# Two-layer mixer network on one core: full-row score corrections, scaling on VectorE alone, a copy moved to ScalarE, and a shorter program end

## The chip, the cores and the metric

The kernel runs on one core of one Trainium2 chip. The metric is the device time of the whole program in microseconds (us). TensorE is called PE here, VectorE DVE, ScalarE ACT, GpSimd POOL, and SyncE, which issues the loads, SP.

## What is computed

256 tokens of width 1024 pass through two layers. Layer 0 mixes the tokens with stick-breaking attention and an S5 state-space model, layer 1 with a sparse attention of 16 heads (4 groups of keys and values, head width 64). After each mixer there is a layer norm, a mixture of 16 experts of which each token uses 2, and another layer norm. The change touches the attention of layer 1:

```
s = q @ ks.T * scale, masked           # "selected" branch, causal here
p = softmax(s);  o_s = p @ vs
s = q @ kw.T * scale, masked           # "window" branch, causal here
p = softmax(s);  o_w = p @ vw
o = g[0] * o_c + g[1] * o_s + g[2] * o_w    # g = sigmoid(gate), one per token, head and branch
out = o @ w_out
```

With 256 tokens every block of 64 keys is selected and the window covers all keys, so both branches are plain causal softmax attention.

## The kernel before

Weights stream from DRAM as tiles of 128x2048 (1 MB) into a pool of `u` buffers, in one fixed order, through SP's DMA queue. A load starts when a `u` buffer is free; the same pool also holds intermediate tiles. The order of instructions on each engine is fixed when the program is built, from the order in which the code issues them and from priorities; at run time each engine executes its own list strictly in order and waits on semaphores for the others.

In `mixer1`, matrices are multiplied in a split form: a value x is written as a rounded part and a remainder, and products of the parts are added. A head has 64 rows (half c of the 128 partitions holds its rounded q, the other half the remainder of q). `kk` holds the rounded keys in both halves, so one matmul over 128 rows adds two of the products, and `kl` the remainders of the keys, in the 64 rows of half c alone. `head(i, c)` does one of 16 heads; i counts eight pairs. For each half t of the queries (128 rows) it takes one PSUM tile `acc` (four of them exist in rotation), and issues three matmuls: q by `kk` (L1504), 64 rows of q by `kl` (L1505), and the causal mask by an identity (L1506). For t = 0 the scores of the two branches are 2 x 128 columns, for t = 1 they are 2 x 256. DVE takes the row maxima (L1507), ACT exponentiates each branch and adds up its rows (L1510), DVE inverts the sums (L1513), multiplies them by the gates (L1515), and the probabilities are scaled: those of t = 0 on DVE (L1522), those of t = 1 on POOL (L1519), by `PSC`.

`turn_p(h)`, two heads later, transposes the scaled probabilities on PE (L1529, L1535) into PSUM tiles `mm`. DVE copies the first (L1530), ACT the second (L1536), into the tile `PT` of the pair, a `u` buffer. `values(i)`, two heads after the second turning, multiplies `PT` by the values (L1550, 16 matmuls), adds the compressed branch (L1553), and ACT and DVE write the two parts of the result to `oT` (L1555, L1556). `attend` interleaves these steps, with other jobs of the layer during the first heads.

At the end of the program (`body`) all engines load a count of tokens (L1726) and pass an `If` (L1728): when an expert has more tokens than fit, the whole network is computed again in a full form. With these inputs the count is below the limit, so each engine jumps over the second network. L1741 in the trace stands for the program's own end.

Of the kernel before, what the change touches and what calls it, by code (L numbers as in the profile page):

```python
# [38 lines left out]
WARM0 = 5  # L39
WARM2 = 2  # L40
LAG = 2
PSC = (lambda h: False, lambda h: True)
OV = 3
LATE = (8, 10)
LATE_S = 11
# [6 lines left out]
class K:  # L52
# [17 lines left out]
    def restart(self, full):  # L70

        self.full = full
        self.plan, self.tiles, self.late, self.late_s, self.in_s, self.last = [], [], [], [], [], []
        self.left = []
        self.issued = self.used = 0
        self.cap = 0
        self.rest = self.n0 = None
        self.mark = None
        self.loads = None
        self.behind = self.cut = self.tail = None  # L80
        self.staged, self.to_split, self.ahead = [], 0, 2
# [49 lines left out]
    def issue(self, cap=None):  # L131

        self.cap = self.cap if cap is None else cap
        while self.issued < len(self.plan):
            if self.issued - self.used - sum(self.used <= i < self.issued for i in self.left) >= self.cap:
                break
            if self.issued in self.left:
                self.tiles.append(None)
                self.issued += 1
                continue  # L140
            t = (self.s if self.issued in self.in_s else self.u)()
            n = 1024 if self.issued in self.last else 2048
            for c in range(0, 2048, n):
                d = self.loads = self.nc.sync.dma_start(t[:, c:c + n], self.plan[self.issued][:, c:c + n])
                if self.mark is not None:
                    self.follow(d, self.mark)
            self.tiles.append(t)
            self.issued += 1

    def issue_late(self):  # L150

        i = self.late.pop(0)
        self.tiles[i] = [self.b2() for _ in range(4)]
        for j, t in enumerate(self.tiles[i]):
            self.nc.sync.dma_start(t, self.plan[i][:, j * 512:j * 512 + 512])

    def issue_s(self):

        i = self.late_s.pop(0)
        self.tiles[i] = t = self.s()  # L160
        self.nc.sync.dma_start(t, self.plan[i])

    def unit(self):
        t = self.tiles[self.used]
# [60 lines left out]
    def pack(self, name, dt, parts, t=None):  # L225

        if t is None:
            t = self.const.tile([P, sum(math.prod(sh) for sh in parts)], dt, name="c_" + name)
            setattr(self, name, t)
        d = self.nc.sync.dma_start(t, self.a[name])  # L230
        if self.loads is not None:
            self.follow(d, self.loads)
        o, r = 0, []
        for sh in parts:
            m = math.prod(sh)
            v = t[:, o:o + m]
            if len(sh) > 1:
                ax = "abcd"[:len(sh)]
                v = v.rearrange(f"p ({' '.join(ax)}) -> p {' '.join(ax)}", **dict(zip(ax, sh)))
            r.append(v)  # L240
            o += m
        return r
# [95 lines left out]
    def ln_transpose(self, li, n, store=None):  # L338

        nc = self.nc  # L340
        hT = self.u([P, KC, T])
        for k in range(KC):
            pt = self.acc() if k in (4, 5) else self.mm()
            for t in range(2):
                nc.tensor.transpose(pt[:, t * P:(t + 1) * P], n[:, t, k * P:(k + 1) * P], self.ident)
            self.scaled(hT[:, k], pt[:, 0:T], li, k, k % 2)
            if store is not None and k % 2:
                nc.sync.dma_start(store[:, k - 1:k + 1], hT[:, k - 1:k + 1])
        return hT

    def scaled(self, o, x, li, k, on_act):
# [305 lines left out]
    def s5_tables(self, load_x, room):  # L657
# [4 lines left out]
        small = lambda t, j: t[:, j * 512:j * 512 + 512].rearrange("p (a r h) -> p a r h", a=NP, r=2)  # L662
        par = us[:, 1344:1392].rearrange("p (x a) -> p x a", x=3)
        c8 = us[:, 1392:1424]
        nc.sync.dma_start(us[:, 1344:1424], self.a["s5_par"])
        load_x()
        bc = ua[:, 0:1024].rearrange("p (x a r h) -> p x a r h", x=2, a=NP, r=2)
        nc.sync.dma_start(bc, self.a["s5_bc"])
        lr, li, ldt = par[:, 0], par[:, 1], par[:, 2]
        cols = us[:, 0:960].rearrange("p (n a) -> p n a", a=NP)  # L670
        ints = us.bitcast(I32)[:, 1424:1456].rearrange("p (n a) -> p n a", a=NP)
# [185 lines left out]
    def s5_kernel(self, ca, bd):  # L857

        nc, s5 = self.nc, self.s5
        nc.gpsimd.memset(bd, 0.0)  # L860
        for g in range(2):
            s = slice(g * 64, g * 64 + 64)
            nc.scalar.activation(bd[s, :, :, g * 16:g * 16 + 16], s5["bb"][s], AF.Copy)
        pk = self.mm()
        for k4 in range(4):
            for ri in range(2):
                for q in range(4):
                    pr = k4 * 4 + q
                    nc.tensor.matmul(pk[q * 32:q * 32 + 32, k4 * P:k4 * P + P], bd[:, pr, ri],
                                     ca[ri][:, pr].rearrange("p d h -> p (d h)"), start=(ri == 0), stop=(ri == 1),  # L870
                                     skip_group_check=True, tile_position=(0, q * 32))
        ks = self.b2([P, 4, P])
        nc.scalar.activation(ks.rearrange("p k n -> p (k n)"), pk, AF.Copy)
        nc.gpsimd.tensor_tensor(ks[:, :, 0:16], ks[:, :, 0:16], self.s5dd, ALU.add)
        kds = []
        for kh in range(2):
            kd = self.drp.tile([16, 16, P], F32, name=f"kd{kh}")
            nc.sync.dma_start(kd.rearrange("h (g k) n -> g h (k n)", g=8),
                                ks[:, kh * 2:kh * 2 + 2].rearrange("p k n -> p (k n)"))
            kds.append(kd)  # L880
        return kds

    def s5_toeplitz(self, kds, kts):

        for kt, kd in zip(kts, kds):
            for j in range(8):
                n = 16 * (8 - j)
                self.nc.sync.dma_start(kt[j * 16:j * 16 + 16, :, P - n:P], kd[:, :, 0:n])

    def s5_transpose(self, x, o):  # L890

# [176 lines left out]
    def mixer0(self):  # L1068
# [5 lines left out]

        def load_x():
            t = self.u()
            half = lambda c: nc.sync.dma_start(t[:, c * 1024:c * 1024 + 1024], self.plan[0][:, c * 1024:c * 1024 + 1024])
            for k in range(0, KC, 2):
                nc.sync.dma_start(xT[:, k:k + 2], self.a["xT"][:, k:k + 2])
                if k == 0:  # L1080
                    half(0)
            half(1)
# [18 lines left out]
        def u_out(j):  # L1101
            def f(ps):
                nc.scalar.activation(uS[:, :, j], ps[:, 0:T].rearrange("p (c i) -> p i c", i=8), AF.Copy)
                if j == 3:
                    ud = self.drp.tile([8, P, P], F32, name="ud")
                    nc.sync.dma_start(ud.rearrange("j a n -> a j n"), uS.rearrange("p j k c -> p j (k c)"))
                    nc.sync.dma_start(U.rearrange("p g k c -> p (g k c)"), ud.rearrange("j (h g) n -> (j h) (g n)", h=16))
            return f

        bbp = [self.u([P, 16, 8, 16]) for _ in range(2)]  # L1110
# [190 lines left out]
    def mixer1(self, hT):  # L1301
# [43 lines left out]
        kk = self.u([P, 2, 2, 2, T], F32R)  # L1345
        vh = self.u([P, 2, 1024])
        V = vh[:, 0].rearrange("p (t n) -> p t n", t=2)
        kl = [self.b2((P, 2, T), F32R) for _ in range(2)]
        rows = (slice(0, 64), slice(64, P))

        turned = {}
# [4 lines left out]
        def k_turn(t):  # L1356
            pt = self.turn(turned["k", t]).rearrange("p (b j) n -> p j b n", b=2)
            n = slice(t * P, t * P + P)
            for c, s in enumerate(rows):
                nc.scalar.activation(kk[s, c, :, :, n], pt[s], AF.Copy)  # L1360
                for j in range(2):
                    v.tensor_tensor(kl[j][s, :, n], pt[s, j], kk[s, c, j, :, n].bitcast(F32), ALU.subtract)
                nc.scalar.activation(kk[rows[1 - c], c, :, :, n], pt[s], AF.Copy)

        js = [self.job_T(xs, window(i)) for i in (1, 2, 3)] + self.jobs_tok(xs, k_out, self.acc)
# [121 lines left out]
        hd = {}  # L1487

        def head(i, c):
            j, s = i // 4, slice(c * 64, c * 64 + 64)  # L1490
            h = i * 2 + c
            if c == 0:
                hd["PT"] = self.u()
            PT = hd["PT"][:, 0:1536].rearrange("p (c b n) -> p c b n", c=2, b=2)[:, c]
# [4 lines left out]
            for t in range(2):  # L1499
# [2 lines left out]
                z3 = z[:, 0:2 * n].rearrange("p (b n) -> p b n", b=2)  # L1502
                q = qq[j][:, c, i % 4, t * P:t * P + P]
                nc.tensor.matmul(z3, q, kk[:, c, j, :, 0:n], start=True, stop=False, skip_group_check=True)  # L1504
                nc.tensor.matmul(z3, q[s], kl[j][s, :, 0:n], start=False, stop=False, skip_group_check=True)  # L1505
                nc.tensor.matmul(z3[:, :, t * P:t * P + P], self.identb, self.caus, start=False, stop=True, skip_group_check=True)  # L1506
                v.tensor_reduce(mx[:, 2 * t:2 * t + 2], z3, AX.X, ALU.max, negate=True)  # L1507
                p_ = self.b2((P, 2, T)) if t else p0
# [2 lines left out]
                                         accum_out=sm[:, 2 * t + b:2 * t + b + 1])  # L1511
                pr.append(p_)
            v.reciprocal(sm, sm)  # L1513
            s2 = sm.rearrange("p (t b) -> p t b", t=2)
            v.tensor_tensor(s2, s2, gt[:, :, h, 1:3], ALU.mult)  # L1515
            for t in range(2):
                x, n, pool = pr[t], P * (t + 1), PSC[t](h)
                if pool:
                    nc.gpsimd.tensor_tensor(x, x, sm[:, 2 * t:2 * t + 2, None].broadcast_to([P, 2, n]), ALU.mult)  # L1519
                    continue  # L1520
                for b in range(2):
                    v.tensor_scalar(x[:, b], x[:, b], sm[:, 2 * t + b:2 * t + b + 1], None, ALU.mult)  # L1522
            hd[h] = (pr, PT)

        def turn_p(h):
            pr, PT = hd[h]
            pt = self.mm()
            for b in range(2):
                nc.tensor.transpose(pt[:, b * P:b * P + P], pr[0][:, b, 0:P], self.ident)  # L1529
            v.tensor_copy(PT[:, :, 0:P], pt[:, 0:T].rearrange("p (b n) -> p b n", b=2))  # L1530
            pt = self.mm()
            for b in range(2):
                for kb in range(2):
# [188 lines left out]
def body(ctx, tc, a, out):  # L1722
# [2 lines left out]
    network(k, a, out)  # L1725
    v = nc.values_load(k.mxi[0:1, 0:1], min_val=0, max_val=T,  # L1726
                       skip_runtime_bounds_check_because="a count of tokens, only compared")
    with tc.If(v > LIMIT):  # L1728

        k.restart(True)  # L1730
        network(k, a, out)
# [20 lines left out]
```

## Time and profile before

| | |
|---|---|
| time, three runs | 756.63, 756.65, 759.73 us (median 756.65) |
| profiled execution | 759.68 us, of which 757.8 us is the span of the trace |
| busy: PE, DVE, ACT, POOL | 733.8 us (97%), 333.1 (44%), 207.5 (27%), 46.8 (6%) |
| granted clock of PE over the span | 0.991 |
| heads of mixer1 in the trace | first score 426 us, last values 495 us |
| matrices moved | 238 MB read, mean 317 GB/s |

The profile gives the busy time of each engine and the share of the span. A busy PE is not a PE at its peak: a matmul counts as busy from its start to its modelled end, and neighbours overlap, so the cost of one is read as the step from the end of the one before it to its own end.

### The profile page before, as it was taken

What the parts mean: (1) busy time and instruction counts of PE and PEld (TensorE: products, weight loads), DVE (VectorE), ACT (ScalarE), POOL (GpSimd) and SP (SyncE); (2) the same over time, 40 slices, a digit from 0 to 9 for tenths busy, and PEclk for the clock granted to TensorE, in tenths of its full rate; (3) what the DMA queues carried; (4) which work ended last, traced back from release to release, by engine and by line L of the source; (5) the groups of instructions that cost most, each with busy time, mean ns of one, the idle gap of its engine ahead of it and who ended that gap; (6) DMA issues with size and microseconds to landing.
All of it is one profiled execution on the core that took longest, in us unless ns stands there. A gap on an engine that the chain in (4) does not pass through costs nothing. (4 is left out here: it accounts for less than half of the span.)

```text
span 757.8 us, 10531 instructions
## 1 busy us (share of the span) xinstructions
PE 733.8 (97%) x4115; PEld 413.9 (55%) x4115; DVE 333.1 (44%) x849; ACT 207.5 (27%) x422; POOL 46.8 (6%) x45
## 2 busy tenths in 40 slices
PE   7999999999999999999999999999999999999993
PEld 6588777634334335334878665687535335343332
DVE  9995667512112112115855897835212112221123
ACT  1345443212101001003534675732211001011002
POOL 2010000002000000000020241300002000000000
PEclk9999999999999999999999998999999999999998
DMA  8838999799999999999982100398799999999941
GB/s 321 299 119 147 398 372 402 256 347 387 381 425 421 421 422 421 420 416 422 420 338 106 57 1 1 135 387 308 233 376 395 393 421 421 422 420 421 421 185 60
DMA packets 42539, 241.00 MB, mean 318 GB/s; under 512 B 8144, under 2 KB 9680, under 8 KB 15568
## 3 DMA queue, kind: packets, MB, share of 16 engines
q1 hardware_dynamic: 42480, 240.23, 80.7%
q8 instruction: 34, 0.56, 0.3%
q14 instruction: 25, 0.20, 0.1%
HBM read 238.38 MB, written 1.84 MB: 317 GB/s over the span
## 5 line engine op out<-in xcount | busy, mean ns | idle before, releaser
L493 PE MATMUL mm<-u,s 128*64 128x512 f32 x960 | 214.3, 595 | 0.0
L493 PEld LDWEIGHTS mm<-u,s 128*64 128x64 f32 x960 | 66.7, 137 | 129.6 <-issue 122.3
L523 PE MATMUL mm<-u,b 128*64 128x512 f32 x512 | 113.1, 593 | 0.0
L528 ACT ACTIVATE b<-mm,gslot 128x512 fp32r<-128x512 f32 x32 | 22.0, 687 | 259.0 <-PE mm L523 259.0
L529 DVE SCALAR_TENSOR_TENSOR b<-mm,gslot,b 128x512 fp32r<-128x512 f32 x32 | 24.0, 751 | 146.2 <-ACT b L528 146.2
L523 PEld LDWEIGHTS mm<-u,b 128*64 128x64 f32 x512 | 36.3, 137 | 72.0 <-issue 70.8
L195 DVE TENSOR_TENSOR s<-u,s 128x1024 fp32r<-128x1024 f32 x37 | 45.8, 1248 | 27.9 <-ACT s L192 26.3
L572 DVE TENSOR_TENSOR b<-b,mm 128x256 f32<-128x256 f32 x32 | 12.0, 417 | 92.0 <-PE mm L493 92.0
L192 ACT ACTIVATE s<-u 128x1024 fp32r<-128x1024 f32 x37 | 38.7, 1056 | 42.0 <-PE acc L205 28.9
L986 PE MATMUL mm<-u,u 128*128 128x256 f32 x208 | 46.7, 382 | 2.5 <-DMA u<-w_in 2.4
L986 PEld LDWEIGHTS mm<-u,u 128*128 128x128 f32 x208 | 38.9, 190 | 9.6 <-issue 2.4
L354 ACT ACTIVATE s<-mm,c_k_all 128x256 f32<-128x256 f32 x32 | 18.1, 564 | 81.8 <-PE mm L469 81.8
L469 PE MATMUL mm<-b,u 128*128 128x256 f32 x160 | 39.0, 325 | 0.0
L203 PE MATMUL acc<-s,u 128*128 128x512 f32 x96 | 38.0, 396 | 0.5 <-ACT u L1206 0.5
L205 PE MATMUL acc<-s,u 128*128 128x512 f32 x96 | 37.8, 394 | 0.0
L204 PE MATMUL acc<-s,u 128*128 128x512 f32 x96 | 37.5, 391 | 0.0
L534 PE MATMUL acc<-b,b 128*128 128x512 f32 x128 | 33.6, 399 | 0.1
L469 PEld LDWEIGHTS mm<-b,u 128*128 128x128 f32 x160 | 29.9, 190 | 6.4 <-issue 4.9
L592 DVE COPY b<-mm 128x512 f32<-128x512 f32 x16 | 11.1, 692 | 46.4 <-PE mm L591 46.2
L356 DVE TENSOR_SCALAR s<-mm,c_k_all 128x256 f32<-128x256 f32 x32 | 16.8, 542 | 22.9 <-PE mm L469 22.7
L534 PEld LDWEIGHTS acc<-b,b 128*128 128x128 f32 x128 | 22.5, 189 | 8.0 <-issue 3.2
L469 PE MATMUL mm<-b,s 128*128 128x256 f32 x96 | 23.5, 286 | 0.0
(312 smaller groups left out, 998.8 us busy)
## 6 DMA issues: line engine op xcount, KB each, us to landing
u<-moe SPq DMA_DIRECT2D x180, 1024.0 KB, 12.5
u<-w_in SPq DMA_DIRECT2D x26, 1024.0 KB, 16.2
u<-w_in SPq DMA_DIRECT2D x10, 512.0 KB, 6.9
s<-moe SPq DMA_DIRECT2D x4, 1024.0 KB, 5.7
b<-moe SPq DMA_DIRECT2D x16, 256.0 KB, 8.1
u<-moe SPq DMA_DIRECT2D x8, 512.0 KB, 16.9
u<-xT SPq DMA_DIRECT2D x4, 256.0 KB, 5.6
out<-u SPq DMA_DIRECT2D x4, 256.0 KB, 4.4
```

What stands on the lines that cost most here:

```text
L192: a = self.nc.scalar.activation(s[:, 0], x, AF.Copy)
L195: self.mark = self.nc.vector.tensor_tensor(s[:, 1], x, s[:, 0].bitcast(F32), ALU.subtract)
L203: mm(o, l[0], r[0], start=first, stop=False, skip_group_check=True)
L204: mm(o, l[0], r[1], start=False, stop=False, skip_group_check=True)
L205: self.tail = mm(o, l[1], r[0], start=False, stop=last, skip_group_check=True)
L469: nc.tensor.matmul(pg[:, 0:T], x[:, t, k * P:(k + 1) * P], g.bitcast(F32) if m == 1 else g, start=(i == 0), stop=(i == 2 * m - 1))
L493: self.mark = nc.tensor.matmul(h[c * 64:(c + 1) * 64], xe[:, k, e + c], w[c], start=(k == 0), stop=(k == KC - 1))
L523: self.mark = nc.tensor.matmul(y[c * 64:(c + 1) * 64], hx[:, f, c * 64:(c + 1) * 64], w[:, c * 512:c * 512 + 512], start=(f == 0), stop=(f ...
L528: nc.scalar.activation(yh, y, AF.Copy, scale=gs)
L529: nc.vector.scalar_tensor_tensor(yl, y, gs, yh.bitcast(F32), ALU.mult, ALU.subtract)
L534: self.tail = nc.tensor.matmul(out[half][t], sT[:, t * P:(t + 1) * P], yy, start=False, stop=(p == 7 and j == 1), skip_group_check=True)
L986: self.mark = self.nc.tensor.matmul(ps, w[:, k * P:k * P + P], xT[:, k], start=(k == 0), stop=(k == KC - 1))
```

## The change

Five edits. (1) `kl` becomes one full `u` tile: like `kk` it has 128 rows for each c, of which POOL sets the 64 rows of the other half to zero, and L1505 multiplies all 128 rows of q. The remainders are formed by four DVE instructions instead of eight. (2) `PSC`, the scaling on POOL and the product of the inverted sums and gates are gone: DVE scales all four blocks of a head, each with two scalars, the inverted sum and the gate. (3) The first turned probabilities are copied to `PT` by ACT instead of DVE. (4) Loads and stores of the full form of the network go through POOL's queue, so that SP has next to nothing in that branch. (5) The `If` no longer prefers to fall through into its body, which puts the block for the other case next after the main program.

```diff
-PSC = (lambda h: False, lambda h: True)
...
         self.full = full
+        self.q = self.nc.gpsimd if full else self.nc.sync
...
-                d = self.loads = self.nc.sync.dma_start(t[:, c:c + n], self.plan[self.issued][:, c:c + n])
+                d = self.loads = self.q.dma_start(t[:, c:c + n], self.plan[self.issued][:, c:c + n])
...
-        kl = [self.b2((P, 2, T), F32R) for _ in range(2)]
+        kl = self.u([P, 2, 2, 2, T], F32R)
+        for c in range(2):
+            nc.gpsimd.memset(kl[(1 - c) * 64:(1 - c) * 64 + 64, c].bitcast(F32), 0.0)
...
-                for j in range(2):
-                    v.tensor_tensor(kl[j][s, :, n], pt[s, j], kk[s, c, j, :, n].bitcast(F32), ALU.subtract)
+                v.tensor_tensor(kl[s, c, :, :, n], pt[s], kk[s, c, :, :, n].bitcast(F32), ALU.subtract)
...
-                nc.tensor.matmul(z3, q[s], kl[j][s, :, 0:n], start=False, stop=False, skip_group_check=True)
+                nc.tensor.matmul(z3, q, kl[:, c, j, :, 0:n], start=False, stop=False, skip_group_check=True)
...
-            s2 = sm.rearrange("p (t b) -> p t b", t=2)
-            v.tensor_tensor(s2, s2, gt[:, :, h, 1:3], ALU.mult)
             for t in range(2):
-                x, n, pool = pr[t], P * (t + 1), PSC[t](h)
-                if pool:
-                    nc.gpsimd.tensor_tensor(x, x, sm[:, 2 * t:2 * t + 2, None].broadcast_to([P, 2, n]), ALU.mult)
-                    continue
                 for b in range(2):
-                    v.tensor_scalar(x[:, b], x[:, b], sm[:, 2 * t + b:2 * t + b + 1], None, ALU.mult)
+                    v.tensor_scalar(pr[t][:, b], pr[t][:, b], sm[:, 2 * t + b:2 * t + b + 1], gt[:, t, h, 1 + b:2 + b],
+                                    ALU.mult, ALU.mult)
...
-            v.tensor_copy(PT[:, :, 0:P], pt[:, 0:T].rearrange("p (b n) -> p b n", b=2))
+            nc.scalar.activation(PT[:, :, 0:P], pt[:, 0:T].rearrange("p (b n) -> p b n", b=2), AF.Copy)
...
-    with tc.If(v > LIMIT):
+    with tc.If(v > LIMIT, preferred_fallthrough_block=False):
```

The order of instructions shifts too. On ACT, between the turning of head 3 and the exponentials of heads 4 and 5, the list reads before (L1510 exponentials, L1536 the copy of the second turned tile, of head 2 at the top and of head 3 at the bottom, L1555 the copy of the first values):

```order
L1536 ACTIVATE u_3196<-mm_3323 128x2x256
L1510 ACTIVATE u_3296,sm_560_3298<-acc_3299,mx_559_3297 128x128 x2
L1510 ACTIVATE b_563_3311,sm_560_3298<-acc_3306,mx_559_3297 128x256 x2
L1555 ACTIVATE u_2877<-mm_3329 128x256
L1510 ACTIVATE u_3296,sm_568_3342<-acc_3343,mx_567_3341 128x128 x2
L1510 ACTIVATE b_571_3355,sm_568_3342<-acc_3350,mx_567_3341 128x256 x2
L1536 ACTIVATE u_3196<-mm_3367 128x2x256
```

and now (L1525 is the new copy, L1531 the old L1536, L1550 the old L1555):

```order
L1525 ACTIVATE u_3193<-mm_3316 128x2x128
L1531 ACTIVATE u_3193<-mm_3320 128x2x256
L1525 ACTIVATE u_3193<-mm_3360 128x2x128
L1531 ACTIVATE u_3193<-mm_3364 128x2x256
L1510 ACTIVATE u_3293,sm_559_3295<-acc_3296,mx_558_3294 128x128 x2
L1510 ACTIVATE b_562_3308,sm_559_3295<-acc_3303,mx_558_3294 128x256 x2
L1550 ACTIVATE u_2874<-mm_3326 128x256
L1510 ACTIVATE u_3293,sm_567_3339<-acc_3340,mx_566_3338 128x128 x2
```

Both copies of head 3 now stand ahead of the exponentials of head 4; before, its one copy stood behind those of heads 4 and 5.

PE, at the same place, turns head 3 and goes on to the scores of head 6. Before (L1529 and L1535 are the turning, `acc_3376` the first scores of head 6):

```order
L1506 LDWEIGHTS c_k_bits
L1506 MATMUL acc_3350<-c_k_bits 128x2x128
L1529 MATMUL mm_3363<-c_k_all,u_3196 128x128 x2
L1535 MATMUL mm_3367<-c_k_all,b_548_3243 128x128 x4
L1504 MATMUL acc_3376<-u_2582,u_2875 128x256
L1505 MATMUL acc_3376<-b_454_2584,u_2875 128x256
```

and now (L1524 and L1530 are the turning):

```order
L1506 LDWEIGHTS c_k_bits
L1506 MATMUL acc_3347<-c_k_bits 128x2x128
L1524 MATMUL mm_3360<-c_k_all,u_3193 128x128 x2
L1530 MATMUL mm_3364<-c_k_all,b_547_3240 128x128 x4
L1504 MATMUL acc_3373<-u_2582,u_2872 128x256
L1505 MATMUL acc_3373<-u_2584,u_2872 128x256
```

The place of the steps is the same; the second score matmul reads a `u` tile instead of a `b2` tile, with 128 rows. Head 6's first scores use the `acc` buffer of head 4's first scores, four tiles earlier.

SP's list ends before with the output DMAs, the load of the count and the jump, behind which the whole second network follows, to row 543:

```order
L348 DMA out<-u_5253 128x512 x4
L1726 TENSOR_LOAD mxi
L1728 COMPARE_AND_BRANCH
L665 DMA u_5312<-s_par 128x80
L1079 DMA u_5306<-xT 128x512
L1077 DMA u_5316<-w_in 128x1024
```

and now:

```order
L348 DMA out<-u_5250 128x512 x4
L1721 TENSOR_LOAD mxi
L1723 COMPARE_AND_BRANCH
L1723 UNCONDITIONAL_BRANCH
L619 COMPARE_AND_BRANCH
L619 UNCONDITIONAL_BRANCH x2
```

No DMA of SP is left behind the jump; its list ends 13 rows later, at row 281.

## Rows read from the trace of the kernel before

**Rows 1.** The page, 40 equal slices of the span: share of the DMA engines.
```profile
DMA  8838999799999999999982100398799999999941
```

**Rows 2.** Windows: busy of PE, PEld, DVE, ACT, POOL, granted clock, DMA share, GB/s.
```profile
440.00:460.00 20.00, 19.00 (x120) 11.68 (x122) 19.45 (x48) 13.51 (x47) 7.35 (x9) 0.95 0.01 2
...
480.00:500.00 20.00, 19.77 (x139) 14.39 (x139) 11.23 (x30) 10.24 (x33) 4.18 (x4) 1.00 0.71 280
```

**Rows 3.** Timeline of PE in mixer1's heads: start, duration, line, out<-in, count.
```profile
468.42 0.50 PE L1505 MATMUL acc<-b,u 64*128 64x512 f32 x1
468.86 0.28 PE L1506 MATMUL acc<-c_k_bits 128*128 128x256 bf16 x1
468.98 0.38 PE L1529 MATMUL mm<-c_k_all,u 128*128 128x128 f32 x2
469.11 0.36 PE L1504 MATMUL acc<-u,u 128*128 128x256 f32 x1
469.41 0.38 PE L1505 MATMUL acc<-b,u 64*128 64x256 f32 x1
469.72 0.66 PE L1535 MATMUL mm<-c_k_all,b 128*128 128x128 f32 x4
470.21 0.27 PE L1506 MATMUL acc<-c_k_bits 128*128 128x256 bf16 x1
470.24 0.47 PE L1504 MATMUL acc<-u,u 128*128 128x512 f32 x1
470.64 0.49 PE L1505 MATMUL acc<-b,u 64*128 64x512 f32 x1
...
471.43 1.52 PE L1550 MATMUL mm<-u,u 128*64 128x256 f32 x16
472.88 0.69 PE L1553 MATMUL mm<-u,b 32*128 32x256 f32 x2
```

**Rows 4.** Timeline of ACT in the same stretch.
```profile
470.41 0.60 ACT L1536 ACTIVATE u<-mm 128x512 f32<-128x512 f32 x1 [1.44 <-PE mm L1535]
470.90 0.36 ACT L1510 ACTIVATE u<-acc,mx 128x128 f32<-128x128 f32 x1
...
471.60 0.47 ACT L1510 ACTIVATE b<-acc,mx 128x256 f32<-128x256 f32 x1
...
472.06 0.46 ACT L1510 ACTIVATE b<-acc,mx 128x256 f32<-128x256 f32 x1
...
473.61 0.38 ACT L1555 ACTIVATE u<-mm 128x256 fp32r<-128x256 f32 x1 [0.99 <-PE mm L1553]
```

**Rows 5.** Timeline of DVE, 447 to 451 us.
```profile
448.11 0.42 DVE L1530 COPY u<-mm 128x256 f32<-128x256 f32 x1
448.45 1.24 DVE L1522 TENSOR_SCALAR u<-u,sm 128x128 f32<-128x128 f32 x2
```

**Rows 6.** Timeline of POOL, the same stretch.
```profile
448.37 1.04 POOL L1519 TENSOR_TENSOR b<-b,sm 128x512 f32<-128x512 f32 x1 [2.03 <-DVE sm L1515]
```

**Rows 7.** Timeline of DVE where POOL is idle.
```profile
466.54 0.19 DVE L1522 TENSOR_SCALAR u<-u,sm 128x128 f32<-128x128 f32 x1
```

**Rows 8.** Windows, columns as in rows 2: the stretch at the lower clock.
```profile
457.40:465.00 7.60, 7.60 (x33) 4.00 (x31) 5.86 (x15) 3.54 (x15) 1.04 (x1) 0.55 0.00 0
```

**Rows 9.** By source line, L348: the four output DMAs on SP.
```profile
L348 SPq DMA_DIRECT2D out<-u x4: 343/376/396, 747.2 to 748.6; - x4
...
DMA to landing us min/median/max: 2.2/4.4/4.5
```

**Rows 10.** By source line, L1728 (the If): sequencer rows of the engines.
```profile
L1728 SPq EVENT_SEMAPHORE  x8: 17/17/17, 753.3 to 753.8; - x8
...
L1728 SPq COMPARE_BRANCH  x1: 50/50/50, 750.0 to 750.0; - x1
```

**Rows 11.** By source line, L1741 (the program's end), 753.2 to 754.2 us.
```profile
L1741 SPq EVENT_SEMAPHORE  x3: 27/28/28, 753.9 to 754.0; - x3
```

**Rows 12.** The same line, 756.2 to 757.0 us.
```profile
L1741 SPq EVENT_SEMAPHORE  x9: 28/28/28, 756.3 to 756.8; - x9
```

More of the change, by code (lines that the diff above doesn't have):

```diff
@@ L154, in issue_late @@
         for j, t in enumerate(self.tiles[i]):
-            self.nc.sync.dma_start(t, self.plan[i][:, j * 512:j * 512 + 512])
+            self.q.dma_start(t, self.plan[i][:, j * 512:j * 512 + 512])
     def issue_s(self):
@@ L160, in issue_s @@
         self.tiles[i] = t = self.s()
-        self.nc.sync.dma_start(t, self.plan[i])
+        self.q.dma_start(t, self.plan[i])
     def unit(self):
@@ L229, in pack @@
             setattr(self, name, t)
-        d = self.nc.sync.dma_start(t, self.a[name])
+        d = self.q.dma_start(t, self.a[name])
         if self.loads is not None:
@@ L347, in ln_transpose @@
             if store is not None and k % 2:
-                nc.sync.dma_start(store[:, k - 1:k + 1], hT[:, k - 1:k + 1])
+                self.q.dma_start(store[:, k - 1:k + 1], hT[:, k - 1:k + 1])
         return hT
@@ L664, in s5_tables @@
         c8 = us[:, 1392:1424]
-        nc.sync.dma_start(us[:, 1344:1424], self.a["s5_par"])
+        self.q.dma_start(us[:, 1344:1424], self.a["s5_par"])
         load_x()
         bc = ua[:, 0:1024].rearrange("p (x a r h) -> p x a r h", x=2, a=NP, r=2)
-        nc.sync.dma_start(bc, self.a["s5_bc"])
+        self.q.dma_start(bc, self.a["s5_bc"])
         lr, li, ldt = par[:, 0], par[:, 1], par[:, 2]
@@ L877, in s5_kernel @@
             kd = self.drp.tile([16, 16, P], F32, name=f"kd{kh}")
-            nc.sync.dma_start(kd.rearrange("h (g k) n -> g h (k n)", g=8),
+            self.q.dma_start(kd.rearrange("h (g k) n -> g h (k n)", g=8),
                                 ks[:, kh * 2:kh * 2 + 2].rearrange("p k n -> p (k n)"))
@@ L887, in s5_toeplitz @@
                 n = 16 * (8 - j)
-                self.nc.sync.dma_start(kt[j * 16:j * 16 + 16, :, P - n:P], kd[:, :, 0:n])
+                self.q.dma_start(kt[j * 16:j * 16 + 16, :, P - n:P], kd[:, :, 0:n])
     def s5_transpose(self, x, o):
@@ L1076, in load_x @@
             t = self.u()
-            half = lambda c: nc.sync.dma_start(t[:, c * 1024:c * 1024 + 1024], self.plan[0][:, c * 1024:c * 1024 + 1024])
+            half = lambda c: self.q.dma_start(t[:, c * 1024:c * 1024 + 1024], self.plan[0][:, c * 1024:c * 1024 + 1024])
             for k in range(0, KC, 2):
-                nc.sync.dma_start(xT[:, k:k + 2], self.a["xT"][:, k:k + 2])
+                self.q.dma_start(xT[:, k:k + 2], self.a["xT"][:, k:k + 2])
                 if k == 0:
@@ L1105, in f @@
                     ud = self.drp.tile([8, P, P], F32, name="ud")
-                    nc.sync.dma_start(ud.rearrange("j a n -> a j n"), uS.rearrange("p j k c -> p j (k c)"))
-                    nc.sync.dma_start(U.rearrange("p g k c -> p (g k c)"), ud.rearrange("j (h g) n -> (j h) (g n)", h=16))
+                    self.q.dma_start(ud.rearrange("j a n -> a j n"), uS.rearrange("p j k c -> p j (k c)"))
+                    self.q.dma_start(U.rearrange("p g k c -> p (g k c)"), ud.rearrange("j (h g) n -> (j h) (g n)", h=16))
             return f
@@ L1489, in head @@
         def head(i, c):
-            j, s = i // 4, slice(c * 64, c * 64 + 64)
-            h = i * 2 + c
+            j, h = i // 4, i * 2 + c
             if c == 0:
```

## The prediction

> **What bounds the kernel now.** I read first where DMA is busy: the slices of the page [rows 1]. Each is 18.9 us. From the 30th on (549 us) the DMA engines are full almost to the end, but in the 22nd to the 25th, about 398 to 474 us, they stand nearly idle: mixer1 holds the `u` buffers, and the loads of the last experts wait for them. So whatever ends mixer1's heads sooner starts that stream sooner, and the end moves by the same amount. Next I read the windows of that stretch [rows 2]: in the heads PE is busy 19.00 and 19.77 of 20 us, DVE 19.45 in the first and 11.23 in the last, ACT 13.51 and 10.24. The stage is therefore PE's, with DVE as a second limit at its start. Last I read the program's end by source line [rows 9 to 12], since PE has finished by 748 us there and the span runs to 757.8.
>
> The profiled execution took 759.68 us, 3.0 above the median of 756.65. The window from 457.4 to 465 us shows PE at a granted clock of 0.55 [rows 8], nearly all of it at the lower of its two levels, 1.2 of 2.4 GHz; 7.6 us at that clock hold about 3.4 us more than the work needs. I take the median as a run without that stretch and make the sum against 756.65.
>
> **Full rows.** A PE step is read from end to end [rows 3]. L1504 with 512 columns ends 0.23 us after the mask matmul before it (470.48 to 470.71); L1505 with the same columns, on 64 rows, ends 0.42 later (to 471.13). For 256 columns it is 0.11 (469.36 to 469.47) against 0.32 (to 469.79). The mask matmul L1506 takes 0.22 behind L1505 (468.92 to 469.14) and 0.10 behind the transposes, which use 128 rows (470.38 to 470.48). So it is the change between 64 and 128 rows that costs, on the way in and back: 0.19 + 0.21 + 2 x 0.12, about 0.6 us a head. With 128 rows throughout I expect L1505 to step like L1504. Sixteen heads: **9.6 us** less work on PE; bounds 0 (the step is due to something else, the load of weights say) and 9.6.
>
> The Trainium skill names this: TensorEngine Tiling (Array Packing), Key Properties, says that changing the tiling mode drains the engine. The trace agrees, with 0.2 and 0.12 us a change.
>
> The cost of the full `kl` lies elsewhere: POOL's two zeroings fall ahead of the heads, where it is all but idle, four wider DVE instructions take the place of eight, and the tile takes one `u` buffer in a stretch where loads are stopped anyway. Nothing, unless a missing buffer makes `PT` wait: with fewer buffers turning over, exponentials of a pair reuse the tile of the second pair back, whose values must be done. That belongs to the next term.
>
> **Scaling on DVE.** The pair of t = 0 scalings took 1.24 us on DVE [rows 5] while POOL held its 1.04 us multiplication [rows 6]; with POOL idle one took 0.19 [rows 7]. So POOL's work is not beside DVE's, it stretches it. Now four scalings of 128, 128, 256 and 256 columns: two at about 0.2, two at 0.3, perhaps 0.1 more with the second scalar; 1.0 to 1.4 us. The small product and the copy of 0.42 go too [rows 5]. DVE sheds 0.5 to 1 us a head, and the probabilities of t = 1 no longer pass through POOL's queue. I count no gain for it: it removes DVE's limit in the first window, and PE's 9.6 can then be had.
>
> **The copy on ACT, and its place.** A copy of 512 columns steps 0.49 (470.41 to 470.90), the two exponentials of t = 0 0.70 (to 471.60), those of t = 1 2 x 0.46, a copy of 256 columns lasts 0.38, some 0.28 as a step [rows 4]. A pair costs ACT now 2 x (0.28 + 0.49 + 0.70 + 0.92) + 0.28 = 5.1 us. PE needs for a head 0.11 + 0.11 + 0.10 + 0.23 + 0.23 + 0.10 = 0.9 for scores and 0.22 + 0.47 = 0.7 for turning (the 0.59 of L1535 there less 0.12 for the change of rows), and for a pair 2.1 for values (471.43 to 473.57) [rows 3]: 5.3 us, where it needed 6.5. So ACT, far from a limit before, comes within 0.2 us of PE, and lists in fixed order that wait for each other can't both be full.
>
> Place one is the stretch shown in the change: ACT has both copies of head 3 ahead of head 4's exponentials, so PE, which has just turned head 3, goes to head 6's scores and finds their buffer waiting for 0.49 + 0.70 us; for t = 1 another 0.92 less 0.32 of own work; for head 7 0.28 + 0.70 less 0.56. Together 1.19 + 0.60 + 0.42 = **2.2 us** of PE standing; up to 3.7 with the handovers and DVE's maxima between.
>
> Place two is every later pair, where copies of heads 8, 10 and 12 stand ahead of exponentials in the same way, but with the 2.1 us of values between, which cover most. I take 0.45 us a pair, between nothing and one group of 0.70 (1.7 where DVE's maxima fall in too): five pairs, **2.3 us**.
>
> The stage gives 9.6 - 2.2 - 2.3 = **5.1 us**.
>
> **The end.** The last output lands at about 748.6 + 4.5 = 753.1 us [rows 9]. SP jumps at 750.0 and does the first wait of the If at 753.3; it spends 0.5 us on eight such waits [rows 10], starts the program's end at 753.9, stands after its third wait from 754.0 to 756.3 with nothing left to wait for, and has done all by 756.8 [rows 11, 12]; the span ends 1.0 later. Now SP's list has no network behind the jump, so 0.5 of waits and 2.3 of standing should go; its jump is short, so some of its waits can be met before 753.1. The floor is the landing at 753.1, a wait or two behind it, and the same 1.0: about 754.4 of the span's 757.8, **3.3 us** less (2.7 if SP starts all its waits at the landing, 0.4 if the standing stays).
>
> The skill's page Runtime: NRT & Kernel Launch, Instruction fetch mechanics, says that a taken branch out of the loaded window forces a fetch. By it SP's two pauses are fetches, and the other engines, which still jump over a whole network, keep theirs. The 3.2 us of SP's jump agrees; no row shows whose fetch the second pause was.
>
> Sum: 756.65 - 5.1 - 3.3 = **748.3 us**. 0.5%, 3.8 us, is about what a measurement of this kernel can tell from no change.
>
> **Rivals.** *PE keeps all of it* (0.22): ACT's copies slip in while PE works on values, and the standing at place one is made up by what DVE gives. That PE has been the fullest [rows 2] speaks for it. 756.65 - 9.6 - 3.3 = 743.8 us. *Forecast* (0.45): 748.3. *ACT eats the stage* (0.19): the queue costs 1.2 us a pair, as much as PE saves, or the 0.19 of L1505 wasn't the rows. For it: 5.1 against 5.3 us a pair. Against: ACT is busy 10 to 13.5 of 20 us now [rows 2]. 756.65 - 3.3 = 753.4 us. *The end hardly moves* (0.10): the second pause comes with any end reached by a jump: 756.65 - 5.1 - 0.4 = 751.2 us. *Slower* (0.04): one loop, copies of a head ahead of exponentials that the PE needs to go on, closes at each of six even heads at 3.7 us instead of once: 22.2 - 9.6 = 12.6, less 3.3: 766 us. It passes 756.65 when a closing costs over (9.6 + 3.3)/6 = 2.2 us. Against it: the values between copy and scores.
>
> **How the numbers follow.** The time is the likeliest case's. The range runs from just under the first rival, 743.5, to 753.0, just short of the third; about half of the third and the slower case lie above, 0.13, and a little below. Faster by over 0.5% (under 752.9): the first, second and fourth case and about a quarter of the third, 0.82. Slower (over 760.4): 0.04. Between: 0.14. A stretch at the lower clock, as in the profiled run, would add about 3 us to a run, not to the forecast.
>
> **What would show it.** After: L1505 stepping 0.22 and 0.11 behind L1504, and the mask 0.1; PE idle before a first score matmul of head 6, released by ACT, for over a microsecond; DVE's window 440 to 460 under 17 us; POOL without work in the heads; a DMA share from 480 to 500 us well over 0.71; the span's end about 1.2 us after the last landing. Wrong if L1505 keeps its step, if PE shows idle time in every pair, or if SP still stands for 2 us at the end.

## The result and the profile after

The changed kernel takes 750.04 us (median of five runs, 749.49 to 751.60); the kernel before took 756.74 us beside it (five runs). The ratio is 0.9899, with a 95% interval of 0.9870 to 0.9927: 1.0% faster, 6.7 us. Forecast were 748.3 us, 8.4 less. The profiled execution took 750.04 us, 748.2 of them span.

Read from the trace, the 6.7 us lie in three places. They are measured between rows that both kernels have: the first score matmul (L1504), the first matmul of the output projection behind the heads (L203), PE's last matmul, the span's end.

| | before | after |
|---|---|---|
| first score | 426.4 | 427.3 |
| first score to output projection | 71.65, of which up to 3.4 are due to the lower clock | 64.66 |
| output projection to PE's last matmul | 249.9 | 249.9 |
| PE's last matmul to the span's end | 9.9 | 6.4 |

The heads give 3.6 to 4.0 us once the stretch at the lower clock [rows 8] is taken off the profiled execution of before (3.4 us by the window, 3.0 by its time against the median), 0.9 is lost ahead of them, and the end gives 3.5. Everything behind the heads has its old length and only moves.

The windows of the heads, columns as in [rows 2], with which they are to be compared:

```profile
440.00:460.00 20.00, 17.49 (x123) 11.06 (x122) 19.28 (x50) 14.79 (x51) 2.78 (x4) 1.00 0.16 53
460.00:480.00 20.00, 19.68 (x151) 13.87 (x150) 17.67 (x58) 17.09 (x67) 0.00 (x0) 1.00 0.00 1
480.00:500.00 20.00, 19.98 (x126) 15.47 (x126) 7.28 (x17) 10.25 (x28) 0.00 (x0) 1.00 0.91 359
```

PE, busy 19.00 us of the first window before, is now busy 17.49: its work shrank and it waits. DVE is as full there as it was, 19.28 for 19.45. The last window shows the stream of weights back earlier, a DMA share of 0.91 for 0.71.

The steps of a head's score matmuls on PE (start, duration; compare [rows 3]):

```profile
475.61 0.60 PE L1530 MATMUL mm<-c_k_all,b 128*128 128x128 f32 x4
475.97 0.36 PE L1504 MATMUL acc<-u,u 128*128 128x256 f32 x1
476.17 0.28 PE L1505 MATMUL acc<-u,u 128*128 128x256 f32 x1
476.29 0.28 PE L1506 MATMUL acc<-c_k_bits 128*128 128x256 bf16 x1
476.33 0.48 PE L1504 MATMUL acc<-u,u 128*128 128x512 f32 x1
476.64 0.40 PE L1505 MATMUL acc<-u,u 128*128 128x512 f32 x1
476.88 0.28 PE L1506 MATMUL acc<-c_k_bits 128*128 128x256 bf16 x1
```

Read from end to end: L1505 ends 0.12 us behind L1504 with 256 columns (476.33 to 476.45) and 0.23 behind it with 512 (476.81 to 477.04), where it took 0.32 and 0.42; the mask matmul L1506 takes 0.12 both times, where it took 0.22. The change between 64 and 128 rows was what cost.

But PE stands where the prediction said it would, at head 6. PE's timeline, with the wait ahead of a row in brackets:

```profile
445.04 0.60 PE L1530 MATMUL mm<-c_k_all,b 128*128 128x128 f32 x4
447.03 0.38 PE L1504 MATMUL acc<-u,u 128*128 128x256 f32 x1 [1.38 <-ACT u L1510]
...
447.94 0.50 PE L1504 MATMUL acc<-u,u 128*128 128x512 f32 x1 [0.29 <-ACT b L1510]
...
448.91 0.39 PE L1504 MATMUL acc<-u,u 128*128 128x256 f32 x1
```

L1530 is the end of head 3's turning. Head 6's first scores then wait 1.38 us for ACT, its second 0.29, head 7's first 0.1; from end to end the three rows take 2.6 us more than their own steps. ACT at that moment:

```profile
445.68 0.60 ACT L1531 ACTIVATE u<-mm 128x512 f32<-128x512 f32 x1
446.17 0.36 ACT L1510 ACTIVATE u<-acc,mx 128x128 f32<-128x128 f32 x1
...
446.86 0.48 ACT L1510 ACTIVATE b<-acc,mx 128x256 f32<-128x256 f32 x1
```

The copy of head 3 (L1531) and at once the exponentials of head 4 (L1510). So far it is the picture that the prediction drew. One view further, DVE:

```profile
445.13 0.41 DVE L1289 TENSOR_TENSOR b<-mm,u 128x256 f32<-128x256 f32 x1
445.46 1.94 DVE L1507 TENSOR_REDUCE mx<-acc 128x2 f32<-128x256 f32 x4
...
448.53 0.59 DVE L1516 TENSOR_SCALAR u<-u,sm,b 128x128 f32<-128x128 f32 x2
449.04 0.73 DVE L1516 TENSOR_SCALAR b<-b,sm,b 128x256 f32<-128x256 f32 x2
449.80 0.18 DVE L1513 RECIPROCAL sm<-sm 128x4 f32<-128x4 f32 x1
```

DVE works until 445.5 us at the rotations of another job (L1286 to L1289, six instructions from 442.9 on, of which the row shows the last), before them at the scaling of heads 2 and 3, and only then takes the maxima of heads 4 and 5, four in a row (L1507 x4). Head 4's scores had been ready since 441. Its first maximum comes at about 445.9, and so its exponentials could have started at most 0.3 us before 446.17, copies ahead of them or not. The named releaser is ACT, the late one is DVE. The two rows of L1516 are the scaling of a head, each read to the start of the next row: 0.51 us for two blocks of 128 columns and 0.76 for two of 256, 1.27 a head.

The end, by source line (L348 the output DMAs, L1723 the If, L1736 the program's end; compare [rows 9 to 12]):

```profile
L348 SPq DMA_DIRECT2D out<-u x4: 344/378/395, 741.2 to 742.6; - x4
...
DMA to landing us min/median/max: 2.1/3.7/4.6
```

```profile
L1723 SPq COMPARE_BRANCH  x2: 38/46/53, 743.9 to 744.0; - x2
```

```profile
L1736 SPq EVENT_SEMAPHORE  x14: 17/28/28, 744.2 to 748.2; - x14
```

SP jumps at 744.0 and is at the waits of the program's end at 744.2 already; what these still wait for is the last landing, at 742.6 + 4.6 = 747.2 us. The span ends 1.0 us later, at 748.2.

### The profile page after: what moved, and what is told of

The parts are those of the page before. It is cut to its first block, busy times and chain, and to the rows that moved or that the text cites. A ratio compares the mean times of both kernels' runs of the same rounds, so it can differ in the third digit from the quotient of the medians.

```text
span 748.2 us, 10487 instructions
## 1 busy us (share of the span) xinstructions
PE 727.4 (97%) x4115; PEld 413.4 (55%) x4115; DVE 328.1 (44%) x845; ACT 212.1 (28%) x438; POOL 32.0 (4%) x31
## 5 line engine op out<-in xcount | busy, mean ns | idle before, releaser
L986 PEld LDWEIGHTS mm<-u,u 128*128 128x128 f32 x208 | 40.5, 197 | 7.5 <-issue 1.7
L203 PE MATMUL acc<-s,u 128*128 128x512 f32 x96 | 38.0, 395 | 0.5 <-ACT u L1206 0.5
```

Of the source, the lines that this page charges most:

```text
L203: mm(o, l[0], r[0], start=first, stop=False, skip_group_check=True)
L986: self.mark = self.nc.tensor.matmul(ps, w[:, k * P:k * P + P], xT[:, k], start=(k == 0), stop=(k == KC - 1))
```

## The experiments

For each, the heads are measured as above, from the first score to the output projection, and the lower clock's share is taken off (windows of half a microsecond, each with its length times one less the granted clock).

| | median us | first score | heads | lower clock | heads without it | PE's end to span's end |
|---|---|---|---|---|---|---|
| before | 756.74 | 426.4 | 71.65 | 3.4 | 68.2 | 9.9 |
| after | 750.04 | 427.3 | 64.66 | 0 | 64.7 | 6.4 |
| rows alone | 755.34 | 427.1 | 66.85 | 1.7 | 65.1 | 10.0 |
| end alone | 753.92 | 426.3 | 71.75 | 3.4 | 68.3 | 6.9 |
| after, copy on DVE | 753.69 | 428.8 | 68.17 | 3.4 | 64.8 | 6.4 |
| after, 64 rows | 758.07 | 426.0 | 73.09 | 3.4 | 69.7 | 6.4 |
| after, ACT's copy twice | 751.69 | 427.5 | 66.23 | 1.7 | 64.5 | 6.9 |
| after, DVE's maxima twice | 759.42 | 426.9 | 72.93 | 5.1 | 67.8 | 6.3 |
| after, t = 1 not scaled | - | 427.2 | 63.28 | 0 | 63.3 | - |
| after, eight subtractions | 751.46 (one) | 427.1 | 66.23 | 1.7 | 64.5 | 6.4 |
| after, ACT scales some | 749.73 | 427.5 | 64.05 | 0 | 64.1 | 6.4 |
| after, POOL scales t = 1 | 750.90 | 427.1 | 65.45 | 0 | 65.5 | 6.9 |
| before, queue alone | 758.14 (one) | 428.1 | 71.69 | 3.4 | 68.3 | 6.8 |
| before, If alone | 758.75 (one) | 426.2 | 68.71 | 0 | 68.7 | 12.0 |

The last row checks the subtraction: its heads have the instructions of before and met no lower clock, and they took 68.7 us where the subtraction gives 68.2 or 68.3 in three other rows. So what has 3.4 us taken off may be half a microsecond too low, and smaller differences between such rows tell nothing.

**Full rows alone.** The kernel before with the full tile, its zeroing and the four wide subtractions that fill it (cut to the lines that matter):

```diff
-        kl = [self.b2((P, 2, T), F32R) for _ in range(2)]
+        kl = self.u([P, 2, 2, 2, T], F32R)      # and its zeroing
...
-                nc.tensor.matmul(z3, q[s], kl[j][s, :, 0:n], start=False, stop=False, skip_group_check=True)
+                nc.tensor.matmul(z3, q, kl[:, c, j, :, 0:n], start=False, stop=False, skip_group_check=True)
```

> The kernel before with only the full-row remainders: POOL and DVE scale, DVE copies, the end as before. Theory (rows change the row group and cost PE 0.6 us a head; the lists' order keeps back part of it): the second score matmul steps 0.12 and 0.23 us, PE's stand before head 6 is small because ACT's copy of head 3 stays behind the exponentials of heads 4 and 5, but DVE, with 1.24 us scalings beside POOL, gives some of it back: 750 to 752 us, 5 to 6.5 less than before. Rival (the stage's gain came from the scaling taken off POOL, or the time is DVE's): at least 755 us.

Measured: 755.34 us, ratio 0.9959 (0.9940 to 0.9978). By the median this is 1.8 us less than before: the theory's 750 to 752 is missed, and the rival's "at least 755" is met. By the trace the heads fall from 68.2 to 65.1, nearly all that the whole change gives them, and 0.7 is lost ahead of them. So one half of the rival falls (the gain didn't come from the scaling taken off POOL, which is still there) and the other stands (the time is DVE's). The window of 440 to 460 and PE's longest waits in the heads (the waiting line, the releaser, us in total, times, longest):

```profile
440.00:460.00 20.00, 16.89 (x115) 10.68 (x116) 19.71 (x48) 12.74 (x43) 7.99 (x9) 0.93 0.16 54
```

```profile
PE acc L1505 <- DVE u L1398: 1.9, 1, 1.9
PE mm L1530 <- DVE u L1523: 1.2, 2, 0.7
```

DVE is busy 19.71 of 20 us, and it is DVE that PE waits for. (L1398 here, L1397 or L1398 in the others, forms the remainders of the queries of heads 8 to 15, which head 8's first scores need.)

**The end alone**, both edits of it (`self.q`, the If).

> The kernel before with only the two edits of the end: POOL's queue for the full form, and the If without preferred fall through. Theory: SP's eight waits and its stand of 2.3 us go, heads unchanged: the span ends about 1.1 us after the last landing, 753.2 us, 3.5 less than before. Rival (the 3.5 seen at the end came with the earlier stream, not with these edits): 756.2 us or more.

Measured: 753.92 us, ratio 0.9961 (0.9938 to 0.9983), 3.2 us less; the heads are those of before to 0.1 us and the end falls from 9.9 to 6.9. The theory holds.

**The copy back on DVE.**

```diff
-            nc.scalar.activation(PT[:, :, 0:P], pt[:, 0:T].rearrange("p (b n) -> p b n", b=2), AF.Copy)
+            v.tensor_copy(PT[:, :, 0:P], pt[:, 0:T].rearrange("p (b n) -> p b n", b=2))
```

> The changed kernel, but DVE makes the copy of the first turned probabilities again. Theory (ACT's two copies of head 3 ahead of head 4's exponentials make PE stand): the list of ACT has the one copy of head 3 behind the exponentials of heads 4 and 5, the stand of 1.38 us before head 6's first scores goes and most of the small waits with it: 747.5 to 748.5 us, faster than the 750.0 of the changed kernel. Rival (DVE is the limit of 440 to 460 us, 19.3 of 20 us busy, and the copy adds 0.33 a head to it): 751 us or more.

Measured: 753.69 us, ratio 0.9932 (0.9908 to 0.9956), slower than the changed kernel; the heads, without the lower clock, take 64.8 us for 64.7. The order that I had made responsible is gone from ACT's list, and nothing is won. The three executions with the highest mean clock (0.998) took 751.2 to 751.6 us, still more than the changed kernel: the rival's 751 or more is met. The window and PE's waits, and ACT's first exponentials of head 4:

```profile
440.00:460.00 20.00, 16.54 (x109) 11.53 (x111) 19.01 (x51) 13.35 (x49) 2.77 (x4) 0.91 0.16 54
```

```profile
PE acc L1504 <- DVE u L1398: 1.2, 1, 1.2
PE mm L1530 <- DVE b L1289: 0.8, 1, 0.8
PE acc L1504 <- ACT u L1510: 0.6, 1, 0.6
```

```profile
447.97 0.37 ACT L1510 ACTIVATE u<-acc,mx 128x128 f32<-128x128 f32 x1 [3.87 <-DVE mx L1507]
```

With no copy of head 3 ahead of them, these exponentials come no earlier, 19.1 us after the first score (18.9 in the changed kernel): ACT stands idle for 3.87 us until DVE's maxima (L1507) are there. PE stands as long, now mostly for DVE. The theory fell. In the profiled execution (754.95 us) the lower clock makes up 5.1 us, 1.7 of them ahead of the heads, which is also why its first score comes so late. Taking all of it off would give 749.8, below those three executions, so the subtraction is too much here.

**64 rows again**, everything else as after.

> The changed kernel with 64-row remainders again, so with scaling on DVE, the copy on ACT and the new end. Theory: the second score matmul steps 0.31 and 0.43 again, the drains fill the time in which PE stood at place one, so that not all of 9.6 us comes back: 753 to 755 us. Rival (ACT sets the pace of the stage, PE's rows are hidden): 750 to 751 us.

Measured: 758.07 us, ratio 1.0006 (0.9988 to 1.0023): slower than either forecast. The heads take 69.7 us, 5.0 more than after and 1.0 to 1.5 more than before. So scaling on DVE and the copy on ACT are no gain by themselves; they lose a good part of the 3.5 us that the end gives, and the lower clock, 3.4 us in this execution, takes the rest. Also, 2.6 us of this execution's time lie outside the span of the trace, where the changed kernel has 1.8; nothing here shows why.

**ACT's copy made twice**, to load ACT alone.

```diff
+            for _ in range(2):
-            nc.scalar.activation(PT[:, :, 0:P], pt[:, 0:T].rearrange("p (b n) -> p b n", b=2), AF.Copy)
+                nc.scalar.activation(PT[:, :, 0:P], pt[:, 0:T].rearrange("p (b n) -> p b n", b=2), AF.Copy)
```

> The changed kernel with the new copy on ACT made twice, the second over the first: 16 times 0.28 us more on ACT, 4.5 us. The heads of the changed kernel take 64.7 us from the first score to the output projection. Theory now (after the run with the copy on DVE gave the same heads, the limit up to 460 us is DVE, not ACT's order): under 1.5 us more, 750 to 751.5. Rival (the place of ACT's copies makes PE stand, as predicted): each loop grows by 0.28 or 0.56, 3 us or more, 753 and up.

Measured: 751.69 us, ratio 0.9917 (0.9890 to 0.9944), 0.2 above the theory's range and 1.3 below the rival's; heads 64.5 us for 64.7.

```profile
PE acc L1504 <- ACT u L1510: 1.6, 1, 1.6
PE acc L1504 <- DVE u L1398: 0.6, 1, 0.6
```

The stand for ACT at head 6 grows from 1.4 to 1.6 us, but the heads don't, once 1.7 us of lower clock are taken off. By the medians, lower clock included, the 4.5 us on ACT cost 1.7 at most (751.69 for 750.04), against 3 or more by the rival.

**DVE's maxima of t = 0 taken twice**, to load DVE alone.

```diff
-                v.tensor_reduce(mx[:, 2 * t:2 * t + 2], z3, AX.X, ALU.max, negate=True)
+                for _ in range(2 - t):
+                    v.tensor_reduce(mx[:, 2 * t:2 * t + 2], z3, AX.X, ALU.max, negate=True)
```

> The changed kernel with DVE's row maxima of t = 0 taken twice: 16 times 0.33 us more on DVE, 5.3 us. Theory (DVE, 19.3 of 20 us busy from 440 to 460, is the limit there and close to it after): 2.5 to 5 us more, 752.5 to 755. Rival (ACT's order is the limit, DVE has room): under 1 us more.

Measured: 759.42 us, ratio 1.0022 (1.0000 to 1.0044); heads 67.8 us, 3.1 more than after for 5.3 us more on DVE. The time is above the forecast, by the lower clock (5.1 us). PE's waits:

```profile
PE acc L1504 <- ACT u L1511: 2.5, 1, 2.5
PE acc L1504 <- DVE u L1398: 2.3, 1, 2.3
```

Here L1511 is the exponentials: PE waits 2.5 us "for ACT" though only DVE was given work, and ACT itself stands 0.53 us for DVE's maxima ahead of these exponentials. This run, the doubled copy and ACT's 3.87 us of idleness with the copy on DVE decide together: up to 460 us, where PE's longer stands lie, DVE sets the pace, not the order of ACT's list.

**Less on DVE.** The scaling of the t = 1 probabilities is left out.

```diff
-            for t in range(2):
+            for t in range(1):
                 for b in range(2):
                     v.tensor_scalar(pr[t][:, b], pr[t][:, b], sm[:, 2 * t + b:2 * t + b + 1], gt[:, t, h, 1 + b:2 + b],
```

> The changed kernel without the scaling of the t = 1 probabilities (so the attention of the second half of the tokens is neither normalised nor gated): 32 scalings of 256 columns less on DVE, about 11 us. Read in the trace alone. Theory (DVE is the limit): the heads take 60 to 62.5 us in place of 64.7 and PE's stands of 440 to 460 us all but go. Rival (ACT's order): 64 to 65 us, with the 1.38 us stand still there.

With these values an expert gets more tokens than fit, so the full form of the network ran behind the first, 11,855 us in all; only the first network is read. Heads: 63.3 us, 1.4 less, and the last values end 60.9 us after the first score where they ended 63.4 after it. The expected 60 to 62.5 is missed; the stand of 1.38 us is gone.

```profile
440.00:460.00 20.00, 18.46 (x143) 12.15 (x143) 16.71 (x42) 16.48 (x54) 2.77 (x4) 1.00 0.11 47
```

```profile
PE acc L1504 <- DVE u L1398: 0.6, 1, 0.6
PE mm L1456 <- DVE u L1398: 0.5, 1, 0.5
```

DVE has fallen to 16.71 us and PE still waits for it at the remainders of the queries (L1398). DVE's busy time in the heads fell by 9.7 us (53.1 to 43.4), and that frees less than half of what 5 us more cost: behind DVE's limit the next one is close. Which it is, this run doesn't show.

**Eight subtractions for four** in forming the remainders.

> The changed kernel with the remainders of the keys formed by eight narrow subtractions instead of four wide ones. The first score comes 0.9 us later in the changed kernel (427.3 for 426.4) and in the one with full rows alone (427.1), behind a stand of PE of 0.65 us at 406 us. Theory (the wide subtractions shift the order of the lists ahead of the heads): first score at 426.4 to 426.6. Rival (it is the u buffer or the zeroing that the full tile takes): 427.1 to 427.4 again.

Measured: first score at 427.1 us. This is the rival's number; the width of the subtractions is not it. Without the full tile the first score comes at 426.0 to 426.4 us, with it at 426.9 to 427.5 (where no lower clock lies ahead of it). The stand itself, in the changed kernel:

```profile
406.28 0.44 PE L1404 MATMUL mm<-c_k_all,b 128*128 128x128 f32 x2 [0.65 <-ACT u L1446]
```

PE has the transposes of the compressed keys (L1404) a few matmuls later in its list than before, behind ACT's copies of values (L1446). What in the full tile moves them, the buffer or the zeroing, was not tried.

**ACT scales t = 0 of eight heads.**

```diff
+            if h < 8:
+                v.tensor_tensor(sm[:, 0:2], sm[:, 0:2], gt[:, 0, h, 1:3], ALU.mult)
+                for b in range(2):
+                    nc.scalar.activation(pr[0][:, b], pr[0][:, b], AF.Identity, bias=0.0, scale=sm[:, b:b + 1])
-            for t in range(2):
+            for t in range(1 if h < 8 else 0, 2):
```

> The changed kernel, but ACT scales the t = 0 probabilities of the first eight heads (with the product of sum and gate made by DVE): DVE loses 16 scalings of 0.34 us and gains 8 products of 0.15, ACT gains 16 of 0.36. Theory (up to 460 us DVE is the limit and ACT has room, since 4.5 us more on ACT cost nothing): the heads take 63 to 64.2 us for 64.7, 748.5 to 749.7 us in all, faster than the changed kernel. Rival (both are full in fixed order, what leaves one burdens the other): 64.5 to 66 us, 750 to 751.5.

Measured: 749.73 us, ratio 0.9890 (0.9857 to 0.9923); heads 64.1. (One of the six executions took 2,748 us, and nothing here says why; the ratio leaves it out, and without it the median is 749.68.)

```profile
440.00:460.00 20.00, 17.40 (x125) 11.45 (x125) 17.96 (x45) 18.56 (x63) 2.84 (x4) 1.00 0.15 53
```

```profile
PE mm L1534 <- DVE u L1555: 1.2, 1, 1.2
```

DVE falls by 1.3 us in the window, ACT rises by 3.8, the heads gain 0.6 us. The direction is the theory's; against the changed kernel's 0.9899 the difference can't be told.

**POOL scales t = 1 again**, the copy stays on ACT.

> The changed kernel with POOL scaling the t = 1 probabilities again, and the copy on ACT. Theory (the 1.04 us on POOL stretch DVE's own scalings by about 0.85 a head, as much as two scalings of 256 columns cost DVE): heads within 1 us of 64.7, 749.5 to 751. Rival (taking POOL out was a gain of its own): 66.5 us or more, 752 and up.

Measured: 750.90 us, ratio 0.9910 (0.9879 to 0.9941); heads 65.5, 0.8 more than after. POOL is busy 20.4 us in the heads for 2.8, and DVE's busy time stays where it was, 53.0 us for 53.1, though 32 scalings left it (and 16 small products came back): what POOL takes off DVE it gives back by stretching it.

**The end's two edits apart**, one execution each.

> The kernel before with only the full form's DMAs in POOL's queue. From PE's last matmul to the span's end the kernel before takes 9.9 us, both edits 6.4 to 6.9. Theory (SP's stands come with the long jump over its list of DMAs): 7.4 us or less. Rival (they come with the block of waits behind the jump, which the other edit moves): 9 us or more.

> The kernel before with only the If that doesn't prefer to fall through. Theory (the long jump stays, SP's list still holds 276 rows behind it): 8.5 us or more from PE's last matmul to the span's end. Rival: 7.4 us or less.

By source line, the queue alone (L1742 the program's end), then the If alone (L1728 the If, L1741 the end):

```profile
L1742 SPq EVENT_SEMAPHORE  x14: 17/28/28, 751.9 to 756.4; - x14
```

```profile
L1728 SPq EVENT_SEMAPHORE  x8: 17/17/17, 747.0 to 750.3; - x8
...
L1728 SPq COMPARE_BRANCH  x2: 38/46/53, 746.9 to 750.4; - x2
```

```profile
L1741 SPq EVENT_SEMAPHORE  x14: 17/28/28, 753.5 to 756.8; - x14
```

With the queue alone PE's last matmul ends at 749.7 and the span at 756.5: 6.8 us, as little as with both edits (6.9 in the run of the end alone). With the If alone it is 744.8 and 756.9: 12.0 us, 2.2 more than before. Both theories hold. SP then makes its eight waits first, up to the landing at 750.2, and makes the long jump after them, from 750.4 to 753.5. The If is harmless only because the queue edit has left SP nothing to jump over and wait for.

## Why the prediction came out as it did

The time lay in the range and 1.7 us above the forecast. By its own steps:

**What bounds the kernel**: right in that whatever ends the heads sooner moves the rest. The output projection comes 6.1 us sooner in the profiled executions (3.0 to 3.4 of them are the lower clock of the one before), and PE's last matmul by the same 6.1. But calling DVE a second limit gave it too little weight: about half of what PE shed came back as standing.

**Full rows, 9.6 us**: right in kind. The steps of L1505 and L1506 add up to 19.5 us before and 10.2 after; 0.9 of the first is the lower clock, so 8.5 us less work on PE. The mask matmul steps 0.12 where 0.10 was taken. The rule of the Trainium skill's page TensorEngine Tiling (Array Packing), Key Properties, that a change of tiling mode drains the engine, agrees with these rows; they show the cost of the change, not the draining itself.

**Scaling on DVE**: the step that failed. The cost of 1.0 to 1.4 us a head was right (1.27), but the conclusion that the edit "removes DVE's limit in the first window" was not: DVE is busy 19.28 of 20 us there. Its busy time in the heads fell from 58.0 to 53.1 us, 0.31 a head where 0.5 to 1 was forecast, and the window that was to fall under 17 us didn't. I had counted the work and not looked at what else stands in DVE's list there, the six rotations ahead of head 4's maxima.

**Place one, 2.2 us**: the stand is there, 2.6 us, and its price came out nearly right by luck, since its cause was wrong. ACT's copies ahead of head 4's exponentials cost 0.3 us at most, since the maxima come no earlier. The copy on DVE and the doubled copy on ACT show it.

**Place two, 2.3 us**: the heads took back 8.5 us less the 3.6 to 4.0 that they gave, 4.5 to 4.9 in all, 1.9 to 2.3 besides place one. The size fits, the account is not shown. PE's wait of 0.7 us at L1398 is no part of it: it lies at 456 us, ahead of these pairs, and the kernel before has it too, longer:

```profile
PE acc L1504 <- DVE u L1397: 1.0, 1, 1.0
```

In the later pairs PE loses 1.1 us ahead of three first score matmuls, at 465.5, 470.2 and 471.2 us; the one wait among them that the profile names is for ACT (0.18 us). The rest is spread over many small steps. ACT's load can't be what sets these pairs, since the doubled copy made them no longer; what does stays open.

**The end, 3.3 us**: 3.5, and 3.0 in the run of the end alone. The mechanism holds, but it is the queue edit that makes it, alone; the If edit alone costs 2.2. The jump over the second network takes SP 3.2 us before [rows 10], 3.1 with the If edit alone, and under 0.2 where SP's list holds no network. The Trainium skill's page Runtime: NRT & Kernel Launch, Instruction fetch mechanics, has a taken branch to code outside the loaded window wait for a fetch; these three numbers agree with it. In the kernel before the jump itself hid behind the last landing (it ended at 753.3, the landing came at 753.1). What went are the 0.5 us of waits and the stand of 2.3 us behind it, and no row shows whose fetch that stand was.

**Not foreseen**: 0.9 us ahead of the heads, which with the heads' 3.6 to 4.0 for 5.1 makes the difference to the forecast. And the rival that the stage would be ACT's falls: 4.5 us more on ACT cost 1.7 at most.

By edit: the full rows alone give 3.1 to 3.6 of the 3.6 to 4.0 us in the heads and cost the 0.7 to 0.9 ahead of them; scaling on DVE and the copy on ACT add half a microsecond on top of them and lose 1.0 to 1.5 without them; the queue edit gives the 3.0 to 3.5 of the end.

What stays open, besides place two, is when the lower clock comes. The changed kernel's five executions (749.5 to 751.6 us) show no gap like that of the kernel before, but five are too few to say that it meets the lower clock less often.

## What to carry to other kernels

Where a wait names an engine, look at what that engine was waiting for before blaming the order of its list; doubling one engine's work at a time tells the real limit cheaply. Keep the rows of neighbouring matmuls the same: here a change between 64 and 128 rows cost 0.2 us on the way in and 0.1 on the way back, 32 times. At the end of a program, give the engine that finishes last as little code as possible to jump over; PE's jump of 4.3 us in the changed kernel costs nothing, since it is over at 746.5, before the last output lands.

## What the hardware showed beyond that

The granted clock falls to 0.5, the lower of its two levels (1.2 for 2.4 GHz), for short stretches in the heads, in nine of the fourteen profiled executions, and each costs 1.7 or 3.4 us. Windows of the version with DVE's maxima doubled:

```profile
448.50:452.00 3.50, 3.08 (x11) 2.19 (x12) 3.25 (x9) 2.98 (x15) 0.00 (x0) 0.56 0.00 0
452.00:459.00 7.00, 5.17 (x41) 3.63 (x39) 6.01 (x19) 5.02 (x21) 0.00 (x0) 0.98 0.01 2
459.00:466.00 7.00, 6.57 (x30) 3.28 (x31) 4.55 (x11) 2.42 (x7) 0.00 (x0) 0.51 0.00 0
466.00:500.00 34.00, 33.80 (x241) 23.46 (x240) 24.95 (x77) 24.77 (x92) 0.00 (x0) 1.00 0.33 127
```

The first fall comes as PE ends a stand of 2.5 us (448.9), the second as it ends one of 2.3 us (459.4). In the other runs with a fall in the heads PE had stood for 0.6 to 1.9 us in the microseconds before it. The reverse does not hold: after the stand of 1.38 us in the changed kernel the clock stayed at 1.00, and after the same stand in the kernel with eight subtractions it fell (449.0 to 452.5 us). Of 30 runs of the kernel before, 19 took 756.0 to 757.7 us and 11 took 759.5 to 761.6, a gap as wide as one such stretch. With edits worth 1 to 4 us a median can move by whether the clock falls; the heads without it are the steadier measure, though the subtraction errs by half a microsecond or more.
